# Three edits of order in one core's hybrid encoder block: z's first SiLU before the decay exponential, a gate row before the last keys, the last token tile of the down projection in halves

## The chip, the cores and the metric

The kernel runs on one core of a Trainium2 chip. The metric is the device time of one execution in microseconds (us); lower is better. The engines are named as in the profile: PE is TensorE (matrix products; PEld is its loading of weights), DVE is VectorE, ACT is ScalarE, POOL is GpSimd, and SP is SyncE, whose queue issues most transfers.

## The reference, cut to what matters

One encoder block over 256 tokens of width 2048. A first stage makes modulation vectors from `c` and normalises `x`. One wide projection of the result `h` feeds two branches, both run in both directions in chunks of 64 tokens: an mLSTM with 4 heads and a gated delta rule (GDN) with 16 heads. The branches are projected, merged with sigmoid gates and projected again, then follows a SwiGLU feed-forward part of 5632 hidden channels and a last RMSNorm.

```python
proj = h @ w_in                    # q, k, v, o of mLSTM; q|k|v, z, beta, decay of GDN; merge gates
log_decay = -exp(A_log) * softplus(a + dt_bias)          # its exponential: the decay factors
o_b = rms_norm(gdn(...)) * silu(z)                       # z's SiLU
g_a, g_b = split(sigmoid(merge), 2)                      # the gate rows
x = x + gate_m * ((g_a * y_a + g_b * y_b) @ w_out)
x = x + gate_f * ((silu(gt) * up) @ w_down)              # w_down: the down projection
return rms_norm(x, norm_final_w)
```

## The kernel before, in words

The 256 tokens are two token tiles of 128. Products run in a split form: a 32-bit operand `a` is taken apart into a high part (`wh`, `hh`: a copy on ACT, L181 or L213, to the type fp32r) and a remainder (`wl`, `hl`: a subtraction on DVE, L183 or L215), and each product is three matmuls, high by high, high by remainder and remainder by high (L186 to L188, L247 to L249).

Two helpers make all the products of the middle. `fjob` (L172) makes 128 output channels by 256 tokens, in two steps of 24 matmuls of 256 columns. `tjob` (L198) makes 2 x 128 tokens by 512 channels; with four pieces of weights these are eight steps of 12 matmuls of 512 columns. Both load weights in pieces of 1 MB through SP's queue into three buffers, and both are generators: each step is one `yield`. When the last step is done, a function `done` takes the result out of PSUM, where four banks (`acc_ps`) serve all jobs and a `tjob` holds two.

The order of the middle is a list. `fills` (L280, filled at L619) begins with z's job for the first four GDN heads (`z_job(0, 2)`), then come the jobs of `rest` (L404): the values `v` of the four mLSTM heads, and then for each i the gate row `mb` of branch b, the output gate `o`, the keys and queries `a_qk` of head i, and the gate row `ma` of branch a. For head 0 only one `a_qk` is in the list, its fourth, since the first three were made with the first stage. The results are kept in DRAM (`keep`, `keep_f`) and read much later by the mLSTM and the merge. `fill(n)` runs n steps from the front of the list, wherever the GDN code leaves room for TensorE. `stream` brings further GDN heads' projections (`b_job`) while two pairs of heads are solved in `gdn_phase2`.

`gates` (L413) computes the scalar gates after the first stage, piece by piece between fills. Its `factors` (L454) makes the exponential of the decay factors, stores them in DRAM and starts loading them back (`decay_load`, POOL's queue) for the first head. It is not called at once but put on the list `behind`, which `settle` (L140) runs at the next weight split. `z_job`'s `done` (L380) puts two SiLUs (one for each token tile) into `sz`.

The instructions of each engine are put in order by a list scheduler, which goes by the order of the code and by when it expects operands to be ready. `order(...)` pins an instruction behind the one traced before it on the same engine; what isn't pinned may move.

In the tail, the down projection (`d0` to `d3`, L1569 on) makes 2 x 128 tokens by 512 output channels each, with 44 blocks of channels to sum over. For `d3`, `by_token` holds the last two splits (four blocks) back, so that token tile 0 ends before token tile 1. `done_d` calls `residual` (L1280: times the gate, plus `x1`, square with a sum) and `finish` (L1548: root, reciprocal, scaling of four groups of 512, stores). The output projection (`o_job`, L1264) has the same tail with the second token tile already in two halves, `parts`: the right half of the last blocks goes to a bank of its own, and `residual` is called with the whole tile for the first half and with `part` for the second.

Of the kernel before, what the change touches and what calls it, by code (L numbers as in the profile page):

```python
# [11 lines left out]
AF = mybir.ActivationFunctionType  # L12
ALU = mybir.AluOpType
# [4 lines left out]
D = 2048  # L18
# [6 lines left out]
KD = 11  # L25
# [27 lines left out]
def hybrid_block(ctx: ExitStack, tc: tile.TileContext, xr, nfr, crow, pk_d, cst_d, ada2, ada4, win0, winb, wint, wba, wbb, wo, wgu, wd, out, dbg=None):  # L53
    nc = tc.nc
    V, S, G, PE = nc.vector, nc.scalar, nc.gpsimd, nc.tensor
# [16 lines left out]
    def order(ins, yes=True):  # L72

        return tc.keep_in_program_order(ins) if yes else ins
# [201 lines left out]
    def run(job):  # L276
        for _ in job:
            pass
# [36 lines left out]
    heads, parts = {}, {}  # L315
# [42 lines left out]
        behind.append(end)  # L358


    szs = {}

    def keep(dst, fn, name):

# [14 lines left out]
    def z_job(g, early=0):  # L379
        def done(ps):  # L380
            szs[g] = evp.tile([P, 2, 512], F32, tag="sz", bufs=1, name=f"sz{g}")
            for t in range(2):
                S.activation(szs[g][:, t], ps[t], AF.Silu)
        return tjob(f"z{g}", [wint[g, u] for u in range(4)], hh, hl, done, early)

    def b_job(h, j):
# [2 lines left out]
    def a_qk(h, j):  # L389
        return fjob(f"a{h}_{j}", winb[36 + 4 * h + j], keep_f(kq_d[h][j], f"a{h}_{j}"))  # L390

    def a_vo(i, h):
        return tjob(
            f"{'vo'[i]}{h}", [wint[4 + 4 * i + h, u] for u in range(4)], hh, hl,
            keep((v_d, o_d)[i][h], (AF.Copy, AF.Sigmoid)[i], f"{'vo'[i]}{h}"),
        )

    def m_job(i, g):
        return tjob(
            f"m{'ab'[i]}{g}", [wint[12 + 4 * i + g, u] for u in range(4)], hh, hl,  # L400
            keep((ma_d, mb_d)[i][g], AF.Sigmoid, f"m{'ab'[i]}{g}"),
        )

    rest = [a_vo(0, h) for h in range(NH_A)]  # L404
    for i in range(4):
        rest += [m_job(1, i), a_vo(1, i)] + [a_qk(i, j) for j in range(4) if i or j == 3] + [m_job(0, i)]

    def evict(o):

# [3 lines left out]
    def gates(w0, zz, first):  # L413
        evict(1)
        order(V.tensor_scalar(zz, first[0], pk[:, PK_GB : PK_GB + 1], sgn, ALU.add, ALU.mult))
        for o in range(2, NP_ + 1):
            evict(o)
        u = w0.tile([P, T], F32, name="u")
        order(S.activation(u, zz, AF.Abs))
        order(S.activation(u, u, AF.Exp, scale=-1.0))  # L420
        gdn_conv(0, 0, None, True)
        yield
        ea = w0.tile([P, 1], F32, name="ea")
        order(S.activation(ea, pk[:, PK_ALOG : PK_ALOG + 1], AF.Exp))
        den = w0.tile([P, T], F32, name="gden")
        order(V.tensor_scalar(den, u, 2.0, None, ALU.add))
        order(V.reciprocal(den, den))
        order(V.tensor_tensor(u, u, den, ALU.mult))
        tr = w0.tile([P, 2, T], F32, name="tr")
        G.memset(tr, 0.0)  # L430
        order(S.activation(tr[0:32, 0], zz[0:32], AF.Sigmoid))
        yield
        yield
        yield
        gdn_conv(0, 1, None)
        yield
        s2 = w0.tile([P, T], F32, name="s2")
        V.tensor_tensor(s2, u, u, ALU.mult)
        poly = w0.tile([P, T], F32, name="poly")
        V.tensor_scalar(poly, s2, 2.0 / 17, None, ALU.mult)  # L440
        for c in (15, 13, 11, 9):
            V.scalar_tensor_tensor(poly, poly, 2.0 / c, s2, ALU.add, ALU.mult)
        yield
        gdn_conv(0, 2, None)
        yield
        for c in (7, 5, 3):
            V.scalar_tensor_tensor(poly, poly, 2.0 / c, s2, ALU.add, ALU.mult)
        V.scalar_tensor_tensor(poly, poly, 2.0, u, ALU.add, ALU.mult)
        sp = w0.tile([P, T], F32, name="sp")
        V.scalar_tensor_tensor(sp, zz, 0.0, poly, ALU.max, ALU.add)  # L450
        V.tensor_scalar(sp, sp, ea, -1.0, ALU.mult, ALU.mult)


        def factors():  # L454
            order(S.activation(s2[32:64], sp[32:64], AF.Exp))
            G.dma_start(alpha_d.rearrange("d h t -> (d h) t"), s2[32:64])
            decay_load(0)

        behind.append(factors)
        yield  # L460

        fi = den
        V.tensor_copy(fi[64:72], sp[96:104])
        mm = w0.tile([P, 2, T + 1], F32, name="mm")
        G.memset(mm[64:72], 0.0)
        R = slice(64, 72)
        V.tensor_tensor_scan(mm[R, 0, 1:], fi[R], zz[R], 0.0, ALU.add, ALU.max)
        V.tensor_tensor_scan(mm[R, 1, 0:T][:, ::-1], fi[R, ::-1], zz[R, ::-1], 0.0, ALU.add, ALU.max)
        ex = w0.tile([P, 2, 3, T], F32, name="ex")
        for v, (cur, prev) in enumerate(((mm[R, 0, 1:], mm[R, 0, 0:T]), (mm[R, 1, 0:T], mm[R, 1, 1:]))):  # L470
            V.tensor_tensor(ex[R, v, 0], fi[R], prev, ALU.add)
            V.tensor_tensor(ex[R, v, 0], ex[R, v, 0], cur, ALU.subtract)
            V.tensor_scalar(ex[R, v, 1], cur, -1.0, None, ALU.mult)
            V.tensor_tensor(ex[R, v, 2], zz[R], cur, ALU.subtract)
            yield

        def weights():
            order(S.activation(ex[R], ex[R], AF.Exp))
            for v in range(2):
                r0 = 64 + 4 * v  # L480
                G.dma_start(mal_d[v], ex[r0 : r0 + 4, v, 0])

        behind.append(weights)
        gdn_conv(1, 0, None)
        yield

        V.tensor_copy(tr[R], ex[R, :, 2])
        V.tensor_copy(tr[96:104], ex[R, :, 1])
        ev0 = w0.tile([P, D + 2], F32, tag="ra", bufs=5, name="ev0")
        for j in range(3):  # L490
            S.activation(ev0[:, j * T : (j + 1) * T], first[13 + j], AF.Copy)
        S.dma_start(kq_d[0][0:3].rearrange("j p t -> p j t"), ev0[:, : 3 * T].rearrange("p (j t) -> p j t", j=3))
        gdn_conv(1, 1, None)
        yield
        ptr = gps("ptr")
        for v in range(2):
            for t in range(2):
                c0 = (v * 2 + t) * P
                PE.transpose(ptr[:, c0 : c0 + P], tr[:, v, t * P : (t + 1) * P], ident)
        V.tensor_copy(bT, ptr[:, 0 : 2 * P].rearrange("p (t c) -> p t c", t=2)[:, :, 0:32])  # L500
        ptv = ptr.rearrange("p (v t c) -> p v t c", v=2, t=2)
        V.tensor_scalar(eT, ptv[:, :, :, 64:72], DK_A**-0.5, None, ALU.mult)
        order(V.tensor_copy(mT, ptv[:, :, :, 96:104]))
        gdn_conv(1, 2, None)
        yield
# [565 lines left out]
    last = (0, 1, 2, 1, 2, 2, 1, 1, 3, 0)  # L1071
# [228 lines left out]
    def token_root(rs, t, part=None):  # L1300

        order(S.activation(rs[:, t : t + 1], rs[:, part or 5 + t :][:, :1], AF.Sqrt, bias=rs[:, 3 + t : 4 + t], scale=1.0 / D))
# [49 lines left out]
    left, right, whole = slice(0, 256), slice(256, 512), slice(0, 512)  # L1352
# [165 lines left out]
    ffh = fp.tile([P, FB, T], F32R, name="ffh")  # L1518
    ffl = fp.tile([P, FB, T], F32R, name="ffl")
    every[0] = 8  # L1520

    for j in range(FB // 4):
# [4 lines left out]
        for e2 in range(2):  # L1527
            px = gps(f"pxf{j}_{e2}")
            for e in range(2):
                f = 2 * e2 + e  # L1530
# [6 lines left out]
    dp = pool(ctx, "dp", side="right")  # L1537
    gf = dp.tile([P, D], F32, name="gf")
# [6 lines left out]
    ss2 = xp.tile([P, 2, 4], F32, name="ss2")  # L1545
    rs2 = xp.tile([P, 8], F32, name="rs2")

    def finish(t):  # L1548

        token_root(rs2, t)  # L1550
        token_rstd(rs2, t)
        r = rs2[:, t : t + 1]
        for g in (2, 0, 3, 1):
            o = x1[:, t, g * 512 : (g + 1) * 512]
            if g == 3:
                order(V.scalar_tensor_tensor(o, o, r, nf[:, 3 * 512 :], ALU.mult, ALU.mult))
            elif g == 2:
                order(V.tensor_scalar(o, o, r, None, ALU.mult))
            else:
                order(S.activation(o, o, AF.Copy, scale=r))  # L1560
        for g in (2, 0, 3, 1):
            c = slice(g * 512, (g + 1) * 512)
            order((S if t and g == 1 else nc.sync).dma_start(out[:, t, c], x1[:, t, c]))
# [5 lines left out]
    for g in range(4):  # L1569
        c = slice(g * 512, (g + 1) * 512)  # L1570

        def done_d(*a, g=g):
            if g == 3:
                residual(a[0], g, a[1], gf, ss2, dp, True, acc=rs2[:, 5 + a[0] : 6 + a[0]])
                finish(a[0])
            else:
                for t, ps in enumerate(a[0]):
                    residual(t, g, ps, gf, ss2, dp)

        run(tjob(f"d{g}", [wd[g, u] for u in range(KD)], ffh, ffl, done_d, by_token=front_d if g == 3 else None))  # L1580
        if g < 3:
            for t in range(2):
                V.tensor_tensor(x1[:, t, c], x1[:, t, c], nf[:, c], ALU.mult)
# [106 lines left out]
```

## Time and profile before

| | us |
|---|---|
| median of 3 runs | 1951.5 |
| lowest and highest | 1947.19, 1954.09 |
| the profiled execution, its time | 1949.33 |
| its span in the trace | 1947.5 |
| PE busy in it | 1919.7 |
| DVE, ACT, POOL busy | 1406.7, 1033.8, 124.1 |

A row of a timeline holds the start in us, the duration in us, engine, line, operation, output<-input with their shapes, how many were merged into the row, and in brackets the idle time of the engine just before and what ended it. `ACT_TABLE_LOAD` is ACT's change to the table of another function. A row of the waits holds who waited for whom, the sum in us, how often, and the longest. A row of a view by windows holds the stretch, its length, and busy time and count for each engine.

### The profile page before, as it was taken

To read this page: it belongs to the slowest core of one execution; us is meant where nothing else is said; L and a number is where in the kernel's file an instruction comes from. 1 tells how busy PE (TensorE), PEld (TensorE's weight loads), DVE (VectorE), ACT (ScalarE), POOL (GpSimd) and SP (SyncE) were. 2 spreads that over 40 slices of the span, in tenths; PEclk is the share of its full clock that TensorE was granted. 3 is DMA by queue.
4 is the path that set the end of the run, shared out by engine and by line. 5 is a ranking of instruction groups with operands and counts; after the bars stand their busy time and mean duration, and the time that the engine had idled before them with its cause. 6 is when DMAs were issued, how large, how long until landed. Compare 5 with 4: busy or idle time off the path is not lost.

```text
span 1947.5 us, 27217 instructions
## 1 busy us (share of the span) xinstructions
PE 1919.7 (99%) x10436; PEld 1699.3 (87%) x10436; DVE 1406.7 (72%) x2084; ACT 1033.8 (53%) x1564; POOL 124.1 (6%) x223
## 2 busy tenths in 40 slices
PE   8999999999999999999999999999999999999997
PEld 6888889998999899889788888888888888888886
DVE  6788886898788789876577988766666565555554
ACT  3147656775776587565544444644444444444443
POOL 0001220111011101120100000200000000000000
PEclk9999999999999999999999999999999999999999
DMA  9997676667676766686777998576667665655563
GB/s 399 420 358 236 188 256 249 214 224 238 219 220 204 241 220 238 208 293 245 268 289 266 351 353 314 195 263 245 246 239 260 239 219 199 204 207 209 196 208 137
DMA packets 80774, 485.68 MB, mean 249 GB/s; under 512 B 11434, under 2 KB 17138, under 8 KB 26626
## 3 DMA queue, kind: packets, MB, share of 16 engines
q1 hardware_dynamic: 64368, 451.02, 63.9%
q0 software_dynamic: 8672, 17.88, 4.3%
q10 hardware_dynamic: 7602, 15.03, 2.0%
q8 instruction: 82, 1.34, 0.3%
q14 instruction: 50, 0.40, 0.1%
HBM read 467.07 MB, written 16.82 MB: 248 GB/s over the span
## 4 chain that ended last, share of the span: by engine, by line
PE 90%; DMA 4%; DVE 3%; ACT 2%; issue 1%; SPq 0%; DVEq 0%; ACTq 0%
PE acc_up L247 4%; PE acc_up L249 4%; PE acc_up L248 4%; PE acc_gt L248 4%; PE acc_d L248 4%; PE acc_gt L249 4%; PE acc_d L247 4%; PE acc_d L249 4%; PE acc_gt L247 4%; DMA ra<-ada 3%; PE acc_b L186 3%; PE acc_o L247 3%; PE acc_o L248 3%; PE acc_o L249 3%; PE acc_b L188 3%; PE acc_b L187 3%
## 5 line engine op out<-in xcount | busy, mean ns | idle before, releaser
L215 DVE TENSOR_TENSOR wl_d<-raw_d,wh_d 128x1024 fp32r<-128x1024 f32 x88 | 107.7, 1225 | 105.9 <-ACT wh_d L213 105.9
L215 DVE TENSOR_TENSOR wl_up<-raw_up,wh_up 128x1024 fp32r<-128x1024 f32 x88 | 107.7, 1225 | 100.7 <-ACT wh_up L213 100.7
L215 DVE TENSOR_TENSOR wl_gt<-raw_gt,wh_gt 128x1024 fp32r<-128x1024 f32 x88 | 107.7, 1224 | 78.6 <-ACT wh_gt L213 78.6
L186 PE MATMUL acc_b<-hh,wh_b 128*128 128x256 f32 x576 | 161.9, 281 | 0.0
L213 ACT ACTIVATE wh_d<-raw_d 128x1024 fp32r<-128x1024 f32 x88 | 92.9, 1056 | 126.5 <-PE acc_d L248 117.7
L188 PE MATMUL acc_b<-hh,wl_b 128*128 128x256 f32 x576 | 158.7, 276 | 0.0
L187 PE MATMUL acc_b<-hl,wh_b 128*128 128x256 f32 x576 | 158.3, 275 | 0.0
L213 ACT ACTIVATE wh_gt<-raw_gt 128x1024 fp32r<-128x1024 f32 x88 | 92.8, 1055 | 117.1 <-PE acc_gt L248 71.1
L213 ACT ACTIVATE wh_up<-raw_up 128x1024 fp32r<-128x1024 f32 x88 | 92.7, 1055 | 108.1 <-PE acc_up L248 77.1
L125 DVE SCALAR_TENSOR_TENSOR ada<-ada,crow 128x2048 f32<-128x2048 f32 x64 | 146.2, 2284 | 0.0
L247 PE MATMUL acc_up<-wh_up,hfh 128*128 128x512 f32 x352 | 133.4, 379 | 0.0
L248 PE MATMUL acc_up<-wh_up,hfl 128*128 128x512 f32 x352 | 133.4, 379 | 0.0
L249 PE MATMUL acc_up<-wl_up,hfh 128*128 128x512 f32 x352 | 133.4, 379 | 0.0
L247 PE MATMUL acc_gt<-wh_gt,hfh 128*128 128x512 f32 x344 | 131.6, 383 | 0.0
L248 PE MATMUL acc_gt<-wh_gt,hfl 128*128 128x512 f32 x344 | 131.3, 382 | 0.2 <-DVE hfl L1475 0.2
L247 PE MATMUL acc_d<-wh_d,ffh 128*128 128x512 f32 x344 | 130.5, 379 | 0.0
L248 PE MATMUL acc_d<-wh_d,ffl 128*128 128x512 f32 x344 | 130.5, 379 | 0.0
L249 PE MATMUL acc_gt<-wl_gt,hfh 128*128 128x512 f32 x344 | 130.4, 379 | 0.0
L249 PE MATMUL acc_d<-wl_d,ffh 128*128 128x512 f32 x344 | 130.4, 379 | 0.0
L595 PE MATMUL first<-x,raw 128*128 128x256 f32 x488 | 110.1, 386 | 6.0 <-ACT x L587 6.0
L595 PEld LDWEIGHTS first<-x,raw 128*128 128x128 f32 x488 | 92.9, 192 | 23.3 <-ACT x L587 10.7
L187 PEld LDWEIGHTS acc_b<-hl,wh_b 128*128 128x128 f32 x576 | 110.6, 192 | 0.1
(403 smaller groups left out, 5294.7 us busy)
## 6 DMA issues: line engine op xcount, KB each, us to landing
ada<-ada SPq DMA_DIRECT2D x64, 1024.0 KB, 5.2
raw_gt<-wgu SPq DMA_DIRECT2D x44, 1024.0 KB, 5.0
raw_up<-wgu SPq DMA_DIRECT2D x44, 1024.0 KB, 5.0
raw_d<-wd SPq DMA_DIRECT2D x44, 1024.0 KB, 4.9
raw_b<-winb SPq DMA_DIRECT2D x36, 1024.0 KB, 5.6
ra<-ada SPq DMA_DIRECT2D x30, 1025.0 KB, 14.9
raw_z<-wint SPq DMA_DIRECT2D x16, 1024.0 KB, 5.0
raw_v<-wint SPq DMA_DIRECT2D x16, 1024.0 KB, 5.4
```

What stands on the lines that cost most here:

```text
L125: order(V.scalar_tensor_tensor(raw, raw, 1.0, row_c[:, :D], ALU.mult, ALU.mult, accum_out=mod[:, c : c + 1]))
L186: PE.matmul(o, wh[:, k], woven(hh[:, kk]), start=kk == 0, stop=False)
L187: PE.matmul(o, wh[:, k], woven(hl[:, kk]), start=False, stop=False)
L188: PE.matmul(o, wl[:, k], woven(hh[:, kk]), start=False, stop=kk == KB - 1)
L213: order(S.activation(wh, raws[u][:, k0 : k0 + 2], AF.Copy), early)
L215: order(V.tensor_tensor(wl, raws[u][:, k0 : k0 + 2], wh.bitcast(F32), ALU.subtract), early or beside[0])
L247: order(PE.matmul(ps[t], xh[:, kk, c], woven(wh[:, k]), start=kk == 0, stop=False), early and steps > 1)
L248: PE.matmul(ps[t], xl[:, kk, c], woven(wh[:, k]), start=False, stop=False)
L249: PE.matmul(ps[t], xh[:, kk, c], woven(wl[:, k]), start=False, stop=kk == last)
L595: PE.matmul(first[o], raw[:, o], x[:, b], start=b == 0 and o % 2 == 0, stop=b == KB - 1 and o % 2 == 1)
```

## The change

Three edits are joined.

1. z's SiLUs for the first four heads are no longer traced when z's job ends; they are kept on a list `opening` and traced at the head of `factors`, in front of the exponential. The second SiLU is pinned behind the first, and the exponential, pinned as before, so stands behind both.
2. In `rest`, for i = 0 alone, the gate row `ma0` comes ahead of the keys `a_qk(0, 3)`; before, it came behind them.
3. In `d3` the second token tile's last four blocks are made in two halves of 256 columns, the right one in a PSUM bank of its own. `residual` is called for the left part with the whole tile and a square of the left half, and for the right part with 256 columns; the two sums of squares are joined through the root's bias by one more small DVE operation before `finish(1)`. `left` and `right` are the slices 0 to 256 and 256 to 512.

```diff
@@ -358,7 +358,7 @@
         behind.append(end)
 
 
-    szs = {}
+    szs, opening = {}, []
 
     def keep(dst, fn, name):
 
@@ -379,8 +379,14 @@
     def z_job(g, early=0):
         def done(ps):
             szs[g] = evp.tile([P, 2, 512], F32, tag="sz", bufs=1, name=f"sz{g}")
-            for t in range(2):
-                S.activation(szs[g][:, t], ps[t], AF.Silu)
+            def silus():
+                for t in range(2):
+                    order(S.activation(szs[g][:, t], ps[t], AF.Silu), not g and t)
+
+            if g:
+                silus()
+            else:
+                opening.append(silus)
         return tjob(f"z{g}", [wint[g, u] for u in range(4)], hh, hl, done, early)
 
     def b_job(h, j):
@@ -403,7 +409,8 @@
 
     rest = [a_vo(0, h) for h in range(NH_A)]
     for i in range(4):
-        rest += [m_job(1, i), a_vo(1, i)] + [a_qk(i, j) for j in range(4) if i or j == 3] + [m_job(0, i)]
+        last = [a_qk(i, j) for j in range(4) if i or j == 3], [m_job(0, i)]
+        rest += [m_job(1, i), a_vo(1, i)] + (last[0] + last[1] if i else last[1] + last[0])
 
     def evict(o):
 
@@ -452,6 +459,7 @@
 
 
         def factors():
+            opening.pop()()
             order(S.activation(s2[32:64], sp[32:64], AF.Exp))
             G.dma_start(alpha_d.rearrange("d h t -> (d h) t"), s2[32:64])
             decay_load(0)
@@ -1547,7 +1555,7 @@
 
     def finish(t):
 
-        token_root(rs2, t)
+        token_root(rs2, t, 7 if t else None)
         token_rstd(rs2, t)
         r = rs2[:, t : t + 1]
         for g in (2, 0, 3, 1):
@@ -1571,13 +1579,23 @@
 
         def done_d(*a, g=g):
             if g == 3:
-                residual(a[0], g, a[1], gf, ss2, dp, True, acc=rs2[:, 5 + a[0] : 6 + a[0]])
-                finish(a[0])
+                t, ps, part = a
+                sq = rs2[:, 5 + t : 6 + t]
+                if not t:
+                    residual(0, g, ps, gf, ss2, dp, True, acc=sq)
+                    finish(0)
+                elif part == left:
+                    residual(1, g, ps, gf, ss2, dp, True, acc=sq, new=left)
+                else:
+                    residual(1, g, ps, gf, ss2, dp, True, part, rs2[:, 7:8], part)
+                    order(V.scalar_tensor_tensor(rs2[:, 4:5], sq, 1.0 / D, rs2[:, 4:5], ALU.mult, ALU.add))
+                    finish(1)
             else:
                 for t, ps in enumerate(a[0]):
                     residual(t, g, ps, gf, ss2, dp)
 
-        run(tjob(f"d{g}", [wd[g, u] for u in range(KD)], ffh, ffl, done_d, by_token=front_d if g == 3 else None))
+        run(tjob(f"d{g}", [wd[g, u] for u in range(KD)], ffh, ffl, done_d, by_token=front_d if g == 3 else None,
+                 parts=((0, slice(0, 512)), (1, left), (1, right))))
         if g < 3:
             for t in range(2):
                 V.tensor_tensor(x1[:, t, c], x1[:, t, c], nf[:, c], ALU.mult)
```

## The prediction

> **What bounds the kernel now.** I read the page first (busy shares and the chain that ended last), then TensorE's own waits, then the timelines of ScalarE (ACT), VectorE (DVE) and TensorE (PE) at the three places that the change touches.
>
> ```profile
> span 1947.5 us, 27217 instructions
> ...
> PE 1919.7 (99%) x10436; PEld 1699.3 (87%) x10436; DVE 1406.7 (72%) x2084; ACT 1033.8 (53%) x1564; POOL 124.1 (6%) x223
> ...
> PE 90%; DMA 4%; DVE 3%; ACT 2%; issue 1%; SPq 0%; DVEq 0%; ACTq 0%
> ```
>
> The reader is to see that 90% of the chain is TensorE, and that TensorE lacks only 1947.5 - 1919.7 = 27.8 us of the span. No edit here takes a matmul away, so a gain can only come out of a place where TensorE stands still, or out of the tail behind its last matmul. TensorE's waits, longest first, hold two entries that lie near the first two edits:
>
> ```profile
> PE p L831 <- DVE pt L823: 1.2, 1, 1.2
> PE acc_v L249 <- DVE wl_v L215: 0.8, 1, 0.8
> ```
>
> All that edits one and two could win directly is therefore 0.8 + 1.2 = 2.0 us, 0.1% of the span. That is the frame of everything below.
>
> **Edit one: z's SiLU ahead of the decay factors' exponential.** The timelines of ACT, PE, DVE and POOL around 156 us, and the line that reads the decay factors:
>
> ```profile
> 153.53 0.40 ACT L354 ACTIVATE vf<-cv 128x256 f32<-128x256 f32 x1
> ...
> 155.16 1.06 ACT L213 ACTIVATE wh_v<-raw_v 128x1024 fp32r<-128x1024 f32 x1 [0.69 <-PE acc_z L248]
> 156.23 1.28 ACT L455 ACT_TABLE_LOAD   x1
> 157.53 0.42 ACT L455 ACTIVATE s<-sp 32x256 f32<-32x256 f32 x1
> 157.96 1.28 ACT L383 ACT_TABLE_LOAD   x1
> 159.26 1.08 ACT L383 ACTIVATE sz<-acc_z 128x512 f32<-128x512 f32 x2
> 160.37 2.00 ACT L213 ACTIVATE wh_v<-raw_v 128x1024 fp32r<-128x1024 f32 x2
> ...
> 170.34 1.28 ACT L478 ACT_TABLE_LOAD   x1
> ```
> ```profile
> 157.55 0.38 PE L249 MATMUL acc_z<-wl_z,hh 128*128 128x512 f32 x1
> ...
> 164.38 0.48 PE L249 MATMUL acc_v<-wl_v,hh 128*128 128x512 f32 x1 [0.84 <-DVE wl_v L215]
> ```
> ```profile
> 163.10 2.35 DVE L215 TENSOR_TENSOR wl_v<-raw_v,wh_v 128x1024 fp32r<-128x1024 f32 x2
> ```
> ```profile
> 163.92 1.49 POOL L330 DMA_DIRECT2D al<-alpha_d  x2 [4.74 <-DMA alpha_d<-s]
> ```
> ```profile
> L653 DVE TENSOR_TENSOR_SCAN dec<-al,cst x64: 393/537/692, 191.4 to 778.6; 128x256 f32<-128x256 f32 x32, 128x128 f32<-128x128 f32 x32
> ```
>
> Before, the functions run SiLU (153.53), Exp, SiLU, Exp (170.34), with a table load of 1.28 us at each turn: three loads. After, they run SiLU, SiLU, Exp, Exp: one load. ACT saves 2 x 1.28 = 2.56 us, but ACT is not what TensorE waits for. What counts is when the third split of v (the ACT row at 160.37) can begin. Before, the exponential and its load (156.23 to 157.95) lay in time when ACT had nothing else to do, because z's last matmul starts only at 157.55 and ends at about 157.93. After z's end stood a load (1.28) and two SiLUs (1.08): 2.41 us until 160.37. After the change the first SiLU can start a little before z's end, since token tile 0 finishes three matmuls before tile 1; behind z's end come the second SiLU (about 0.6, half of the 1.08), the load (1.28) and the exponential (0.42), 2.3 us. So the split begins at about 160.2 instead of 160.37: the load has only changed its place, from in front of the SiLUs to in front of the exponential. That is -0.1 us.
>
> TensorE's 0.84 us at 164.38 does not hang on that split (done by 161.4) but on DVE, which takes up the matching remainder only at 163.10, behind the scans of the mLSTM gates. DVE's order comes from a list scheduler, and a split ready 0.2 us earlier may or may not move the remainder ahead of one of those small operations. Ends: 0 and -0.84. I take -0.1, nearest to the row that says how far the split moves.
>
> The change makes Exp wait for z's end. Queued behind it on ACT is the third split, already counted. On POOL's queue the store of the decay factors and both loads wait for it: the exponential moves from 157.53 to about 159.9, the loads at 163.92 to about 166.3, and the first scan that reads them comes at 191.4. That slack of some 20 us covers 2.4 us. The second load saved (170.34) frees ACT at a place where TensorE shows no wait. Cost there: nothing.
>
> [...]
>
> **Edit two: the first kept gate row (ma0) ahead of the last keys of head 0.** TensorE's matmuls of ma0 in two stretches, ACT around its eviction, DVE, and the readers of both products:
>
> ```profile
> 294.00:316.00 22.00, 15.71 (x72) 13.53 (x72) 0.00 (x0) 1.00 0.76 276
> ...
> 359.00:366.00 7.00, 5.43 (x24) 4.46 (x24) 0.00 (x0) 1.00 0.93 258
> ```
> ```profile
> 295.18 0.59 ACT L368 ACTIVATE ev_o<-acc_o 128x512 f32<-128x512 f32 x1
> ```
> ```profile
> 364.93 1.28 ACT L368 ACT_TABLE_LOAD   x1
> 366.23 1.08 ACT L368 ACTIVATE ev_ma<-acc_ma 128x512 f32<-128x512 f32 x2
> 367.33 1.28 ACT L678 ACT_TABLE_LOAD   x1
> ...
> 368.63 0.26 ACT L678 ACTIVATE nn<-vps,epsc 128x4 f32<-128x4 f32 x1
> ```
> ```profile
> 371.44 0.35 DVE L706 SCALAR_TENSOR_TENSOR mi<-ks,sm,dec 128x128 f32<-128x128 f32 x1 [1.75 <-PE ks L701]
> ...
> 374.30 0.65 DVE L823 TENSOR_TENSOR pt<-p,cst 128x512 f32<-128x512 f32 x1
> ```
> ```profile
> L1165 SPq DMA_DIRECT2D gta<-ma_d x4: 327/327/424, 1040.8 to 1111.3; - x4
> ```
> ```profile
> L988 POOL DMA_DIRECT2D mkq<-kq_d x4: 756/757/766, 843.9 to 960.4; - x4
> ```
>
> ma0 now has six of its eight steps (72 matmuls of 12 each) by 316, pauses for 43 us, and gets the last two (24) at 359. With two keys' steps moved behind it, it fills eight steps in a row and is done by 315; the keys take the two steps at 359. The number of steps, the order of SP's weight loads (one 1 MB piece for two steps in both kinds) and every later job stay. The gate's two sigmoids (1.08) move to 315, where the table of o0's sigmoid (295.18) is still in, so both loads (2 x 1.28) go: 3.64 us of ACT leave the stretch at 365. Its two stores move along; their readers come at 843.9 and 1040.8 or later, hundreds of us off.
>
> What does TensorE get from it? ACT's root at 368.63 would come some 3 us earlier, but the operation that needs it, DVE's at 371.44, waited for TensorE's ks, not for it. Then DVE does eleven operations up to 374.30 before it reaches pt, and that is TensorE's 1.2 us. All of this is DVE's order and TensorE's order, which the edit does not touch. So I take 0, with the ends -1.2 (DVE finds room for pt earlier) and +0.6 (at 315 the sigmoids stand in front of a weight split for the next head, half of their 1.08 uncovered).
>
> **Edit three: the last token tile of down in halves.** DVE and ACT in the tail, then the same construction where the kernel already has it (output projection), and a two-operand operation of 256 elements elsewhere:
>
> ```profile
> 1937.18 0.16 DVE L1305 RECIPROCAL rs<-rs 128x1 f32<-128x1 f32 x1 [1.12 <-ACT rs L1302]
> ...
> 1937.78 0.74 DVE L1556 SCALAR_TENSOR_TENSOR x<-x,rs,nf 128x512 f32<-128x512 f32 x1
> 1938.45 0.68 DVE L1285 TENSOR_TENSOR tmss<-acc_d,gf 128x512 f32<-128x512 f32 x1
> 1939.16 0.69 DVE L1288 TENSOR_TENSOR x<-x,tmss 128x512 f32<-128x512 f32 x1
> ```
> ```profile
> 1939.89 0.63 ACT L1289 ACTIVATE tmss<-x 128x512 f32<-128x512 f32 x1 [1.17 <-DVE x L1288]
> ...
> 1940.64 0.29 ACT L1302 ACTIVATE rs<-rs 128x1 f32<-128x1 f32 x1
> ```
> ```profile
> 1233.19 0.42 DVE L1285 TENSOR_TENSOR tmss<-acc_o,gm 128x256 f32<-128x256 f32 x1 [0.26 <-PE acc_o L272]
> ...
> 1233.92 0.71 DVE L1288 TENSOR_TENSOR x<-x,tmss 128x256 f32<-128x256 f32 x1
> ```
> ```profile
> 1234.66 0.42 ACT L1289 ACTIVATE tmss<-x 128x256 f32<-128x256 f32 x1 [0.32 <-DVE x L1288]
> ...
> 1235.20 0.29 ACT L1302 ACTIVATE rs<-rs 128x1 f32<-128x1 f32 x1
> ```
> ```profile
> 140.94 0.42 DVE L428 TENSOR_TENSOR u<-u,gden 128x256 f32<-128x256 f32 x1
> ```
>
> The second tile's multiplication at 1938.45 has no idle time in front of it: it did not wait for TensorE but for DVE, which was closing the first tile. Every instruction there is pinned behind the one traced before it, and the first half's residual is traced behind `finish(0)`. So the half that TensorE now delivers early finds DVE in the same state, free at 1938.45. And the first half is not a half on DVE: `residual` is called with `part` at its default, so it multiplies and adds all 512 columns (the right ones incomplete), and only the square is narrowed. From 1938.45 to the start of the root:
> - before: 0.71 (multiplication, start to start) + 0.73 (addition, to ACT's start) + 0.75 (square to root) = 2.19;
> - after: 0.71 + 0.62 (addition, 0.69 less the 0.07 by which independent operations overlap, as at 1937.78) + 0.44 + 0.44 (multiplication and addition of 256: 0.42 each, 0.02 between dependent ones) + 0.54 (square of 256 to root, 1234.66 to 1235.20) = 2.75.
>
> That is **+0.56 us**. The combining of the two sums (one 128x1 operation on DVE) runs while ACT squares. Twice as many, half as wide matmuls end TensorE hardly later, with more than 1 us until DVE asks. If the addition takes the 0.71 of 1233.92 (where POOL worked beside it) it is +0.85. If DVE could use the 1.12 us of idle time in front of 1937.18 for the first residual, the root would come 0.5 us earlier instead. I take +0.56.
>
> [...]
>
> **The sum.** -0.1 + 0 + 0.56 = about +0.4 on the profiled execution's 1949.33 (span 1947.5). Its time lies 2.2 below the median of 1951.5; on the median the forecast is **1951.9 us**, no change.
>
> **Rivals.**
> - *Both stalls go and the tail's idle time is used:* -0.84 - 1.2 - 0.5 = -2.5, so 1949.0. For it: DVE's order is made anew, and ACT loses four table loads. Against it: neither stall has ACT as its releaser, and the tail's order is pinned. Chance 0.18.
> - *ACT's queue is blocked, slower:* the pinned pair of SiLUs is put ahead of v's split at 155.16. ACT then stands until z's end, the split moves to 158.5, 3.4 late, its remainder (1.2) ends at 160.8 or later instead of about 158.4, and TensorE needs it near 160.8. From about 2.5 us of lateness on, each us is TensorE's: 0.9 there, 0.9 more at the next split behind Exp, and the tail's 0.56: +2.4, so 1953.9. For it: only the exponential pinned that split's place before. Against it: the split is ready earlier than z's end. Chance 0.14.
> - *The change does not do what it says:* the second tile does not begin earlier, since finish(0) is in front. That is my forecast for edit three, and needs no other time.
> - *The scheduler re-sorts other stretches:* the direction is open, 1951.9 with some us either way. Chance 0.08.
>
> My forecast has the remaining 0.60.
>
> **How the numbers follow.** The three runs of before spread from 1947.19 to 1954.09, so a median of a few runs lies within some 3 us of its true place. The range runs from the faster rival less 2.5 to the slower one plus 2.6: 1946.5 to 1956.5. About 0.3%, 5.9 us, is what a measurement of this kernel can tell from no change. The faster rival with all of the spread, and half of the re-sorting, give 0.04 for faster; the slower rival with the spread and the rest of the re-sorting give 0.08 for slower; 0.88 is left for the same.
>
> **What would show it.** Edit one right: one table load between 153 and 172 instead of three, exponential near 159.9, TensorE's wait near 164.4 still there. Wrong: that wait gone or over 1.5 us. Edit two right: ma0's sigmoids near 315 with no load, no load between 364 and 368, pt's wait still about 1.2. Edit three right: the second tile's multiplication starts right behind the first tile's closing, and from there to its root takes about 2.75 instead of 2.19. The forecast is wrong if TensorE's idle time between the first and the last matmul changes by more than 2 us.

## The result: 2.9 us faster, where no change was forecast

| kernel | median | runs | ratio to the kernel before (95% interval) |
|---|---|---|---|
| before | 1950.54 us (1946.09 to 1954.73) | 20 | |
| after | 1948.22 us (1944.16 to 1949.96) | 20 | 0.9985 (0.9978 to 0.9992) |

The ratio stands for -2.9 us (-1.6 to -4.3). The gain is smaller than the 0.3% that was called measurable, but it is beyond its interval, and the median forecast of 1951.9 is missed by 3.7 us. A later set of runs of the same kernel gave 1947.50 us against 1950.70, ratio 0.9980 (0.9971 to 0.9989).

The profiled execution of after took 1949.13 us, 0.9 above its own median, and only 0.2 less than the profiled one of before. So the two profiles hardly differ in length, and what changed has to be read place by place. Its page:

```profile
span 1947.3 us, 27241 instructions
...
PE 1920.5 (99%) x10448; PEld 1701.7 (87%) x10448; DVE 1407.8 (72%) x2087; ACT 1029.1 (53%) x1562; POOL 124.1 (6%) x223
...
PE 91%; DMA 4%; DVE 2%; ACT 2%; issue 1%; SPq 0%; DVEq 0%; ACTq 0%
```

TensorE still sets the time. ACT has 1033.8 - 1029.1 = 4.7 us less work, close to four table loads (4 x 1.28 = 5.1). TensorE's own waits between 200 and 900 us:

```profile
PE vps L674 <- ACT vf L354: 1.5, 2, 0.8
PE vps L676 <- ACT sqkq L671: 1.2, 1, 1.2
PE acc_z L249 <- DVE wl_z L215: 0.9, 1, 0.9
PE p L864 <- DVE pt L853: 0.7, 1, 0.7
PE pb L888 <- DVE r L889: 0.4, 2, 0.2
```

Both waits that the prediction named, for wl_v near 164 and for pt near 374, are gone. In their place stand 1.2 us for sqkq (222 us; 0.3 in before), 0.7 for another pt (328 us), and a second wait for vf (398 us).

### The profile page after: what moved, and what is told of

Read it like the earlier page. It is cut to its first block, busy times and chain, and to the rows that moved or that the text cites. A ratio compares the mean times of both kernels' runs of the same rounds, so it can differ in the third digit from the quotient of the medians.

```text
span 1947.3 us, 27241 instructions
## 1 busy us (share of the span) xinstructions
PE 1920.5 (99%) x10448; PEld 1701.7 (87%) x10448; DVE 1407.8 (72%) x2087; ACT 1029.1 (53%) x1562; POOL 124.1 (6%) x223
## 4 chain that ended last, share of the span: by engine, by line
PE 91%; DMA 4%; DVE 2%; ACT 2%; issue 1%; SPq 0%; DVEq 0%; ACTq 0%
PE acc_up L247 4%; PE acc_up L249 4%; PE acc_up L248 4%; PE acc_gt L248 4%; PE acc_d L248 4%; PE acc_gt L249 4%; PE acc_d L247 4%; PE acc_d L249 4%; PE acc_gt L247 4%; DMA ra<-ada 3%; PE acc_b L186 3%; PE acc_o L247 3%; PE acc_o L248 3%; PE acc_o L249 3%; PE acc_b L187 3%; PE acc_b L188 3%
## 5 line engine op out<-in xcount | busy, mean ns | idle before, releaser
L186 PEld LDWEIGHTS acc_b<-hh,wh_b 128*128 128x128 f32 x576 | 110.6, 192 | 0.1
```

Source lines behind the costliest of these rows:

```text
L186: PE.matmul(o, wh[:, k], woven(hh[:, kk]), start=kk == 0, stop=False)
```

## The experiments

The first four kernels take the three edits apart: each alone, and the first two together. The diffs are the hunks of the change itself. Two theories were held against each other: that each edit acts where it stands ("local"), and that the list scheduler sorts distant stretches anew, so that waits at 492 and 805 us go. Before, run beside them, had a median of 1950.0 us.

| run | median | ratio (95% interval) |
|---|---|---|
| e1_silu_alone | 1949.65 us | 0.9995 (0.9986 to 1.0004) |
| e2_gate_row_alone | 1948.71 us | 0.9993 (0.9984 to 1.0002) |
| e3_halves_alone | 1950.92 us | 1.0000 (0.9987 to 1.0012) |
| e12_without_halves | 1947.10 us | 0.9985 (0.9976 to 0.9993) |

> Edit one alone. In the profile of the changed kernel TensorE's wait for wl_v near 164 (1.0 us lost) is gone, and two waits far from the edits are gone too: wl_a near 492 (1.38) and wl_z near 805 (1.05). Local theory: each edit works only where it stands, so here only the wait near 164 goes: about -1.0 us, and the waits near 492 and 805 stay. Re-sorting theory: edit one shifts the list scheduler's expected times, and far places are put in another order; then one or both of the waits near 492 and 805 go here, -2 to -3.4 us, or they appear in the run of edit two alone. Forecast on record: -0.1 us.

> Edit two alone. Local theory: the wait for pt near 373 (1.34 us lost) goes, ACT's two table loads near 365 go, the wait near 164 stays, and nothing changes at 492 and 805: about -0.5 to -1.3 us. Re-sorting theory: the waits near 492 and 805 go here if they don't in the run of edit one alone: -2 to -3 us. Forecast on record: 0.

> Edit three alone. Both theories: every instruction before the last product keeps its place; the second tile's root comes 0.4 to 0.6 us later after the start of its multiplication (2.75 instead of 2.19), and the time rises by about 0.5 us, which lies at the edge of what the comparison can tell. Rival: the halves shorten the tail, about -0.5 us.

> Edits one and two without the halves of edit three. If the halves cost about 0.5 us as forecast, this is that much faster than the changed kernel, about -3.4 us against the kernel before (the changed kernel: -2.9, interval -1.6 to -4.3). If the halves gain, it is slower than the changed kernel. If the waits at 492 and 805 need only one of the edits, the stretch from 0 to 930 us ends as early as in the run of that edit alone plus the local gain of the other.

No edit alone could be told from no change; the first two together could. In these traces, the wait near 164 is missing wherever the SiLU edit is made and the wait near 374 wherever the gate row is moved. The wait at 492 us is missing in the trace of e3 too, whose program there is that of before: it belongs to one execution, and the re-sorting theory loses its best piece of evidence.

### Where the SiLU edit gets its microsecond: e5_split_behind_exp

Timelines of ACT and DVE in the kernel after:

```profile
157.20 0.60 ACT L384 ACTIVATE sz<-acc_z 128x512 f32<-128x512 f32 x1 [0.74 <-PE acc_z L249]
157.69 1.05 ACT L213 ACTIVATE wh_v<-raw_v 128x1024 fp32r<-128x1024 f32 x1
158.64 0.59 ACT L384 ACTIVATE sz<-acc_z 128x512 f32<-128x512 f32 x1
159.24 1.28 ACT L463 ACT_TABLE_LOAD   x1
160.54 0.42 ACT L463 ACTIVATE s<-sp 32x256 f32<-32x256 f32 x1
```
```profile
160.46 1.23 DVE L215 TENSOR_TENSOR wl_v<-raw_v,wh_v 128x1024 fp32r<-128x1024 f32 x1
```

Only the second SiLU is pinned. The list scheduler put v's third split between the two, at 157.69 instead of 160.37, and DVE took up its remainder at 160.46, in the middle of the gates' small operations, instead of 163.10. Is it this order, or simply the saved load? The experiment pins the split behind the exponential and leaves the saving:

```
+  PIN = ("v0", 1, 0)
...
-  order(S.activation(wh, raws[u][...], AF.Copy), early)
+  order(S.activation(wh, raws[u][...], AF.Copy), early or (name, u, k0) == PIN)
```

> The SiLU edit alone, with v's third split held behind the exponential on ScalarE; the table load that the edit saves stays saved, and the exponential and decay loads stay early. Theory 'the split between the two SiLUs' (in the kernel after, the list order put v's third split ahead of the exponential, and VectorE's remainder of it between the scans): TensorE's wait near 164 comes back at 0.6 to 1.0 us, since the remainder is late again; z's last matmul to v's first 100 matmuls as in the kernel before. Rival 'the saved load' (ScalarE simply is 1.3 us earlier): the wait stays away, under 0.2 us, and acc_v stands 1.0 us or more ahead of before. Time: within 1.5 us of before by either, so the rows decide and not the median.

```profile
157.27 1.25 ACT L385 ACTIVATE sz<-acc_z 128x512 f32<-128x512 f32 x2 [0.73 <-PE acc_z L250]
158.54 1.28 ACT L463 ACT_TABLE_LOAD   x1
159.83 0.42 ACT L463 ACTIVATE s<-sp 32x256 f32<-32x256 f32 x1
160.27 2.00 ACT L214 ACTIVATE wh_v<-raw_v 128x1024 fp32r<-128x1024 f32 x2
```
```profile
163.07 2.35 DVE L216 TENSOR_TENSOR wl_v<-raw_v,wh_v 128x1024 fp32r<-128x1024 f32 x2
```
```profile
164.34 0.48 PE L250 MATMUL acc_v<-wl_v,hh 128*128 128x512 f32 x1 [0.85 <-DVE wl_v L216]
```

Both table loads that the edit saves are still saved (of before's four, at 156.23, 157.96, 170.34 and 173.13, two are left, at 158.54 and 171.81), the split comes at 160.27 (160.37 before), DVE makes both remainders one behind the other at 163.07, and TensorE waits its 0.85 us. So at this wait the order wins the time and the loads win none. The times are too near to say it for the whole kernel (1949.02 us, ratio 0.9997, 0.9985 to 1.0009; e1 has 0.9995).

### Where part of it goes again: e7_silu_no_decay_loads

At 178 us TensorE stands 1.2 us ahead of before, and near 222 it waits for sqkq, which on ACT stands behind a split that waits for a 1 MB piece of v's weights. The same row of ACT's timeline, first in before, then in the kernel after, in a second execution of it (e9), and in a kernel with the same two edits (e8):

```profile
222.58 1.06 ACT L213 ACTIVATE wh_v<-raw_v 128x1024 fp32r<-128x1024 f32 x1 [2.31 <-PE vps L668]
```
```profile
222.34 1.06 ACT L213 ACTIVATE wh_v<-raw_v 128x1024 fp32r<-128x1024 f32 x1 [3.25 <-DMA raw_v<-wint]
```
```profile
221.64 1.06 ACT L213 ACTIVATE wh_v<-raw_v 128x1024 fp32r<-128x1024 f32 x1 [2.67 <-DMA raw_v<-wint]
```
```profile
220.76 1.06 ACT L213 ACTIVATE wh_v<-raw_v 128x1024 fp32r<-128x1024 f32 x1 [1.81 <-DMA raw_v<-wint]
```

The piece lands when it lands: the last three, with the same order of work up to there, are 1.6 us apart. The experiment takes two other transfers away from the stretch: it fills the decay rows of heads 2 and 3 with zeros and leaves their loads out.

```
-  order(G.memset(al[:, :, 0:8], 0.0))
-  order(G.dma_start(al[:, :, 8:], alpha_d[:, h].partition_broadcast(P)))
+  order(G.memset(al if h in (2, 3) else al[:, :, 0:8], 0.0))
+  if h not in (2, 3):
+      order(G.dma_start(al[:, :, 8:], alpha_d[:, h].partition_broadcast(P)))
```

> The SiLU edit alone, with the two decay-row broadcasts of heads 2 and 3 (256 KB each, issued near 204 and 212) replaced by zeros, which leaves out those heads' decay rows; the order of instructions on every engine is that of the edit alone. Theory 'v's weights land no earlier' (the gain of 1 us at 164 is given back near 222 because a 1 MB piece of v's weights lands at 221.6 to 222.3 whatever TensorE's lead is, behind the broadcasts' traffic): with the traffic gone the piece lands early, the wait of 1.2 us near 222 shrinks under 0.4, and TensorE stands 0.9 to 1.3 us ahead of before at 260. Rival 'the piece is asked for late' (its issue waits for VectorE's remainder, which has not moved): the wait near 222 stays at 0.9 us or more.

```profile
220.11 1.06 ACT L213 ACTIVATE wh_v<-raw_v 128x1024 fp32r<-128x1024 f32 x1 [1.15 <-issue]
```

No DMA wait is left, TensorE loses less than 0.1 us there, and at 252 us it stands 1.9 us ahead of before (e1: 0.2; after: 0.2). The traffic theory holds: how much of edit one survives goes by when this piece lands, and the loads around 204 to 220 us make it late (with them ACT waited 1.81 to 3.25 us for it in the last three executions above, without them not at all in e7). They need not cost anything: in e8, which has both, the split starts at 220.76 and TensorE loses under 0.15 us there as well. (1948.86 us, 0.9995, 0.9985 to 1.0005.)

### Why the wait for pt goes: e6 and e10

ACT of before behind ma0's eviction, and DVE behind pt; then the same two engines in the kernel after:

```profile
369.44 2.95 ACT L181 ACTIVATE wh_b<-raw_b 128x1024 fp32r<-128x1024 f32 x3
```
```profile
374.87 2.34 DVE L183 TENSOR_TENSOR wl_b<-raw_b,wh_b 128x1024 fp32r<-128x1024 f32 x2
```
```profile
365.31 1.04 ACT L181 ACTIVATE wh_b<-raw_b 128x1024 fp32r<-128x1024 f32 x1
...
368.65 1.06 ACT L181 ACTIVATE wh_b<-raw_b 128x1024 fp32r<-128x1024 f32 x1 [1.00 <-PE acc_mb L248]
```
```profile
367.08 1.22 DVE L183 TENSOR_TENSOR wl_b<-raw_b,wh_b 128x1024 fp32r<-128x1024 f32 x1
...
369.74 1.23 DVE L183 TENSOR_TENSOR wl_b<-raw_b,wh_b 128x1024 fp32r<-128x1024 f32 x1 [0.76 <-ACT wh_b L181]
```

Queued behind the sigmoids and their loads were three weight splits of the next head. Without them the first of the three comes 4.1 us earlier (365.31) and the second some 1.7, DVE makes their remainders in time in which it was idle, and the scheduler can put 48 matmuls of acc_b between the two short stretches of p (373.80 to 379.24). pt is as late as ever (374.97; 374.30 in before); TensorE has something else to do. Two kernels keep ma0's job at its old place. e6 evicts it without a Sigmoid:

```
-  keep((ma_d, mb_d)[i][g], AF.Sigmoid, ...)
+  keep((ma_d, mb_d)[i][g], AF.Sigmoid if i or g else AF.Copy, ...)
```

> The kernel before with the first kept gate row (ma0) evicted by Copy instead of Sigmoid, at its old place near 365: it leaves ma0's sigmoid out, so two table loads (2.6 us of ScalarE) near 365 go, while the job keeps its place in the list. Theory 'what stood behind the loads' (the next head's weight splits waited behind them, and with them the matmuls that could cover pt's lateness): TensorE's wait of 1.3 us near 373 goes, and the waits near 328 (0.9) and 335 (0.4) that the moved row brought do not appear; time 1.0 to 2.0 us under before, apart from waits elsewhere that differ from run to run by about 1 us. Rival 'the place of the row' (only the job's new place in the list frees the matmuls): the wait near 373 stays at 0.8 us or more, and the time is within 0.7 us of before.

e10 keeps Sigmoid and both loads, and issues ma0's eviction from the list that each split empties, five splits on, which puts it behind two of the next head's splits on ACT:

```
-  for t in range(2):
-      S.activation(ev[:, t], ps[t], fn)
+  def out():
+      ...
+      for t in range(2):
+          order(S.activation(ev[:, t], ps[t], fn), name == "ma0")
...
+  def wait(n):
+      behind.append((lambda: wait(n - 1)) if n else out)
...
+      wait(5)
```

> The kernel before with one thing changed: the eviction of the first kept gate row (with its Sigmoid and both table loads) stays in the same job at the same place of the list, but is issued behind two of the next head's weight splits on ScalarE instead of ahead of them. No table load is saved. Theory 'the splits behind the loads': TensorE's wait of 1.3 us near 373 goes (under 0.2) though the loads are all still there, and no waits come near 328 and 335; the remaining price is the wait near 398 (0.9 instead of 0.2), so 0.6 to 1.5 us under before. Rival 'the loads' time' (ScalarE lacks 2.6 us near 365, whatever stands first): a wait of 0.7 us or more stays between 366 and 380, and the time is within 0.5 us of before.

```profile
364.35 1.04 ACT L181 ACTIVATE wh_b<-raw_b 128x1024 fp32r<-128x1024 f32 x1
...
367.52 1.06 ACT L181 ACTIVATE wh_b<-raw_b 128x1024 fp32r<-128x1024 f32 x1 [1.32 <-PE acc_mb L248]
368.59 1.28 ACT L369 ACT_TABLE_LOAD   x1
```

The stretch from 372 to 378 us of PE, in before, after and e10 (the first two numbers: length, busy time of PE):

```profile
372.00:378.00 6.00, 4.77 (x41) 1.00 0.36 124
```
```profile
372.00:378.00 6.00, 6.00 (x53) 1.00 0.67 224
```
```profile
372.00:378.00 6.00, 6.00 (x57) 1.00 0.84 290
```

The wait is gone in both (in e6 too the stretch is 6.00 of 6.00 us), so neither the row's place nor the loads' time made it: it was that the splits were queued behind the loads. e6: 1948.03 us, ratio 0.9989 (0.9978 to 1.0000). e10: 1948.39 us, ratio 0.9987 (0.9978 to 0.9997).

The moved row has a price that these two do not pay. A split on ACT and this head's pt on DVE in before, then, in the kernel after, ACT and DVE ahead of the wait at 328 us:

```profile
318.74 1.06 ACT L181 ACTIVATE wh_b<-raw_b 128x1024 fp32r<-128x1024 f32 x1 [2.62 <-PE acc_b L187]
```
```profile
327.60 0.69 DVE L845 TENSOR_TENSOR pt<-p,cst 128x512 f32<-128x512 f32 x1
```
```profile
314.22 0.60 ACT L368 ACTIVATE ev_ma<-acc_ma 128x512 f32<-128x512 f32 x1 [1.00 <-PE acc_ma L249]
...
321.93 1.06 ACT L181 ACTIVATE wh_b<-raw_b 128x1024 fp32r<-128x1024 f32 x1
```
```profile
323.02 2.59 DVE L183 TENSOR_TENSOR wl_b<-raw_b,wh_b 128x1024 fp32r<-128x1024 f32 x2 [3.46 <-ACT wh_b L181]
...
325.92 2.28 DVE L125 SCALAR_TENSOR_TENSOR ada<-ada,crow 128x2048 f32<-128x2048 f32 x1
...
328.53 0.68 DVE L853 TENSOR_TENSOR pt<-p,cst 128x512 f32<-128x512 f32 x1
```

The sigmoids now stand at 314, a split that before had at 318.74 comes at 321.93, DVE does two remainders in one piece ahead of the 2.28 us of ada, and this head's pt comes at 328.53 instead of 327.60. Measured as matmul starts later than their usual pitch (0.11 us apart for 256 columns, 0.22 for 512), TensorE loses 0.87 us at 328 that it does not lose in before. The 0.36 at 335 is no added price: it stands in place of 0.38 that before, e6, e10 and e11 lose at 343 to 344. At 398, where TensorE now arrives earlier than vf, it loses 0.93 instead of 0.22, and this price e6 (0.93) and e10 (0.74) pay too. From 252 to 452 us the moved row therefore wins nothing: in the five traces that have it (e2, after, e9, e12, e8) the matmul at 452 comes 0.05 us later on average (-0.25 to +0.24), measured from the one at 252 and against before. In e6, e10 and e11, where only the splits come earlier, it comes 1.1 to 1.4 us earlier.

### What the moved row does win: spells of half clock

TensorE's granted clock falls to about 0.5 for 3.4 us (in e10 and e12 once for 6.8) at a few places, not in every execution. Behind the wait for pt, in e3 (the clock is third from the right):

```profile
375.30:378.70 3.40, 3.40 (x18) 3.37 (x18) 3.40 (x5) 1.45 (x7) 2.50 (x6) 0.53 0.36 55
```

Three of the five traces that have that wait (e3, e5 and e7; not before and e1) show this spell, and none of the eight without it. e3 and e5 lie 1.2 and 1.6 us behind before at 389 us, though they were 0.2 and 0.1 us ahead at 252, a loss of 1.4 and 1.7; half of 3.4 is 1.7, and the stretch above holds 18 matmuls where before, at clock 1.00, has 31. The mean clock of whole runs says the same with more weight. Kernels with the wait: 0.99635 over 142 runs; without it: 0.99695 over 99; the difference has a standard error of 0.00011. One spell is worth 0.5 x 3.4 / 1947 = 0.00087, so the kernels without the wait have 0.7 of a spell less, about 1.2 us. This mean does not say where a spell falls, and away from 375 us the traces do not differ that way: there the five with the wait have 1.8 windows of half clock each ahead of the tail, the eight without it 2.1. That the wait brings on the spell is inferred from this company, not shown by a run that adds a wait alone.

### What belongs to one execution: e9_after_again

The kernel after, unchanged:

> The kernel after once more, unchanged: which waits belong to its program and which to one execution. Theory 'far waits are chance': TensorE's waits near 328 (0.9), 335 (0.4), 398 (0.9) and 578 (0.9) come again within 0.1 us and those near 163 and 373 stay away; those near 222, 446, 805 and 978 and the places of the half-clock spells differ from the first execution by 0.3 us and more in two of the four or more. Rival 'all waits belong to the program': all within 0.1 us. Time 1948.2 by the earlier median.

Matmul starts against their usual pitch, worked out from the traces:

| TensorE's lost time near | after | after again |
|---|---|---|
| 222 us (weights of v land late) | 1.40 | 0.81 |
| 328, 335 | 0.87, 0.37 | 0.86, 0.36 |
| 398 | 0.93 | 0.92 |
| 446 | 1.02 | 1.20 |
| 805 | under 0.1 | 1.45 |
| 979 | 0.69 | 0.28 |

and the stretch around 945 us, first in after, then in its second execution:

```profile
944.10:947.50 3.40, 3.40 (x6) 1.34 (x5) 0.20 (x2) 1.63 (x2) 0.03 (x1) 0.51 0.90 320
```
```profile
944.10:947.50 3.40, 3.40 (x13) 1.91 (x13) 0.59 (x6) 1.81 (x3) 1.15 (x2) 1.00 0.97 333
```

328, 335 and 398 come again to 0.01 us, and 446 to 0.2; 222, 805 and 979 do not. The first execution has spells of half clock near 944 and near 1009 (0.51 and 0.52), the second has neither (1.00 at both). The two executions of one program are 2.6 us apart in span (1947.3 and 1944.7), as much as the whole change is worth. The wait of 1.2 us for wl_a in before (492 us) is of this kind as well: of thirteen traces only before and e10 have it.

### The tail: e8_without_halves_tail_in_gaps and e11_best_of_the_runs

DVE and ACT at the end of the kernel after:

```profile
1937.12 0.75 DVE L1564 SCALAR_TENSOR_TENSOR x<-x,rs,nf 128x512 f32<-128x512 f32 x1
1937.79 0.68 DVE L1293 TENSOR_TENSOR tmss<-acc_d,gf 128x512 f32<-128x512 f32 x1
1938.51 0.69 DVE L1296 TENSOR_TENSOR x<-x,tmss 128x512 f32<-128x512 f32 x1
1939.11 0.42 DVE L1293 TENSOR_TENSOR tmss<-acc_d,gf 128x256 f32<-128x256 f32 x1
1939.57 0.43 DVE L1296 TENSOR_TENSOR x<-x,tmss 128x256 f32<-128x256 f32 x1
```
```profile
1940.57 0.29 ACT L1310 ACTIVATE rs<-rs 128x1 f32<-128x1 f32 x1
```

From the second tile's multiplication to its root: 1940.57 - 1937.79 = 2.78 us, against 2.19 before. From the first tile's multiplication (1933.99) to that root it is 6.58 us in after and e3 and 6.57 in e9, and 5.99 in before and e12: the halves cost 0.59 us in every trace. In e8 the two edits stay and the tail is written in another order: the first tile's reciprocal and its two closings on ACT come between the left half's multiplication and its addition, its two closings on DVE behind the right half's addition. The halves' matmuls are as in the change (cut, and with short lines joined):

```
+  def begun():
+      token_rstd(rs2, 0); close(0, (0, 1)); send(0, (0, 1))
...
   if not t:
       residual(0, ...)
-      finish(0)
+      token_root(rs2, 0)
   elif part == left:
-      residual(1, ..., new=left)
+      residual(1, ..., new=left, between=begun)
   else:
       residual(1, ..., part, rs2[:, 7:8], part)
+      close(0, (2,))
       order(V.scalar_tensor_tensor(rs2[:, 4:5], ...))
-      finish(1)
+      close(0, (3,)); send(0, (2, 3))
+      token_root(rs2, 1, 7); token_rstd(rs2, 1)
+      close(1, (2, 0, 3, 1)); send(1, (2, 0, 3, 1))
```

> The SiLU and gate row edits, with the halves in another order on VectorE and ScalarE: the left half's multiplication and addition go ahead of the first token's closing multiplications, into VectorE's idle time behind the first token's residual, and the first token's two closings on VectorE go behind the right half's addition, into the time in which ScalarE squares. Theory 'VectorE's queue sets the tail': from the first token's residual's multiplication to the second token's root 5.3 us instead of 6.6 (after) and 6.0 (before); the span's end 1.2 to 1.6 us nearer to the last matmul than in the kernel before, and the time 1.0 to 1.8 us under that of the same two edits without halves (near 1945.6). Rival 'the writes at the end set it' (the last two writes share the queues): under 0.4 us.

```profile
1931.04 0.69 DVE L1293 TENSOR_TENSOR tmss<-acc_d,gf 128x512 f32<-128x512 f32 x1 [2.80 <-PE acc_d L272]
1931.77 0.69 DVE L1296 TENSOR_TENSOR x<-x,tmss 128x512 f32<-128x512 f32 x1
1932.38 0.69 DVE L1293 TENSOR_TENSOR tmss<-acc_d,gf 128x512 f32<-128x512 f32 x1
1933.57 0.16 DVE L1313 RECIPROCAL rs<-rs 128x1 f32<-128x1 f32 x1 [0.50 <-ACT rs L1310]
```
```profile
1935.93 0.29 ACT L1310 ACTIVATE rs<-rs 128x1 f32<-128x1 f32 x1
```

The left half's multiplication now lies in the idle time ahead of the first tile's reciprocal (0.50 us of it are left instead of 1.11), and from the first multiplication to the second tile's root it is 4.89 us: 1.1 less than before and 1.7 less than after, a larger gain than the expected 5.3 us would have been. The kernel took 1945.09 us, ratio 0.9974 (0.9964 to 0.9984). That is two microseconds under e12, but each was measured beside other runs of before, and the two intervals overlap; the 1.1 us of the trace is what is shown of the tail.

The last kernel joins the SiLU edit, e10's splits and this tail:

> The SiLU edit, the gate row's eviction behind two weight splits (its job at the old place of the list), and the tail with the halves in VectorE's gaps. Theory: as the earlier run with the row moved and the same tail (1945.1 us), without the waits that the moved row brought near 328 (0.9) and 335 (0.4): 0.5 to 1.3 us under it, about 1944.2. Rival 'another wait takes their place' (the list is sorted anew): within 0.4 us of 1945.1 or above it.

It took 1945.21 us, ratio 0.9971 (0.9961 to 0.9980), and beats both kernels; beside it after had 1947.50 and before 1950.70. Between e8 and e11 no difference can be told, so the 0.5 us or more that was to come on top is not shown, though the 0.87 us at 328 is gone from its trace.

## Why the prediction was wrong

**Edit one, -0.1: the price was too small, and the reason weak.** The prediction saw that the wait hangs on DVE's order, named -0.84 as an end, and took -0.1 "nearest to the row that says how far the split moves". The split did not move by 0.2 but by 2.7 us (160.37 to 157.69), because only the second SiLU is pinned and the split fits between the two; so the remainder moved too. The wait went whole: TensorE is 1.1 us ahead at 178. At 252, measured from z's last matmul and against before, 0.1 to 1.6 us of it are left in six traces with the edit (e1, after, e9, e12, e8, e11), 0.8 on average. The exponential "near 159.9" was nearly right (160.54). Of loads there are two from 153 to 172 us and not one: at 159.24, and at 170.62 the return to SiLU, which before makes at 173.13. The saving is the two loads that were forecast, and e5 shows that they are worth nothing at this wait, as the prediction said.

**Edit two, 0: the step that failed is "All of this is DVE's order and TensorE's order, which the edit does not touch".** It touched both. The prediction followed the root and the chain to pt, and did not count what else stood behind the loads on ACT: the three weight splits at 369.44, whose matmuls could stand in front of pt's. The end of +0.6 for sigmoids in front of a split at 315 was right in kind: there it cost 0.87. Up to 452 us the sum of the two is near nothing, so the 0 stands by luck; the win, as far as the clock shows it, is the spell that no longer follows the wait, about 1.2 us. That a wait of 1.2 us can be followed by a spell of half clock, 1.4 and 1.7 us of loss in e3 and e5, was nowhere in the sum.

**Edit three, +0.56: right.** 2.78 us against the forecast 2.75, by the mechanism given; in the times a cost of 0.59 cannot be told (e3's ratio is 1.0000, 0.9987 to 1.0012), as expected of its size.

**The rivals.** "Both stalls go" (chance 0.18) is what happened, with its -2.5 near the measured -2.9, though its part on the tail's idle time did not; that part needed e8's order. That the two numbers lie so near is luck: the tail cost 0.59 where this rival let it win 0.5, and what the end of pt's wait won was lost again at 328 and 398. "ACT's queue is blocked" did not occur: the split at 155.16 stayed at 155.04. "The scheduler re-sorts other stretches" holds for 328 us; the differences at 222, 492, 805, 944 and 1009 us, which look like it, change from one execution to the next.

**The sum.** Edit one 0.8, the spared spells 1.2, the halves -0.6: 1.4 us faster. Measured are 2.9 (1.6 to 4.3), and 3.9 (2.1 to 5.7) in the later set of runs. The first two edits without the halves give 2.0 by this sum and 2.9 (1.4 to 4.7) by measurement. The sign agrees, but 1.4 lies below both intervals: 1.5 to 2.5 us have no place in the trace to which they could be put. The record gives span and granted clock of every run, so the mean span can be parted into what half clock took, span x (1 - clock), and the rest. Against before the rest is -2.0 us in e1, -0.5 in e2, +0.4 in e3 and -2.3 in the later runs of after; the clock's part is +0.8, -1.2, +0.1 and -1.7 (standard errors 0.4 to 0.6 throughout). So the gate row's gain does lie in the clock, and what is missing seems to lie with the SiLU edit, of whose 2.0 the traces place 0.8. Where the remainder of it arises stays open.

## What to carry to other kernels

- When work is taken off an engine that is not the bound, list everything queued behind it up to the next wait, and ask which of it the bound engine could use as filling: the gain can lie in matmuls that become available, and not in the chain that ends at the wait.
- With a list scheduler, a freed slot is filled: an instruction that is not pinned can move by far more than the time that was saved, and a price can appear at another place (the moved row's stands at 328 us, 45 us ahead of the wait that it ends).
- Before a wait in one trace is explained, look at whether it comes again in a second execution of the same program; here two executions of one kernel were 2.6 us apart, as much as the change.

## What the runs showed of the hardware

- Spells of half clock last 3.4 us (0.51 and 0.53 over such windows, in after at 944.10 and in e3 at 375.30) or, seen twice (e10 and e12), 6.8. The one at 375 us goes with 1.4 and 1.7 us that e3 and e5 lost against before from 252 to 389 us. Spells come and go between executions of one program (after has those near 944 and 1009, its second execution neither). A wait of 1.2 us among short matmuls (eight of p in 0.98 us ahead of it, eight in 1.08 behind) was followed by a spell in three of five traces, and the eight traces without the wait have none there. What sets a spell off is not shown.
- A split that waited for a 1 MB piece of weights started 1.6 us apart in three executions with the same order of work (220.76 to 222.34), while another queue, POOL's, brought decay rows; with two of those loads left out (e7, one execution) no wait for the piece was seen, and the split started at 220.11.
